# Splits of activations in two steps, scaled groups straight to their parts, and TensorE's operands low in SBUF

## The chip, the core and the metric

The kernel runs on one core of a Trainium2 chip. The metric is the device time of one execution in microseconds (us), the median of several runs. TensorE does the matmuls (PE in the rows), VectorE (DVE) and ScalarE (ACT) work on tiles, GpSimd (POOL) and SyncE (SP) issue DMAs. SBUF is the memory on the chip (128 partitions), PSUM the small memory into which TensorE writes, here as eight banks of 128x512 numbers.

## The reference

One layer for 256 tokens of 2048 features, in float32:

```
h = x + 0.5 * ffn1(rms_norm(x))            # ffn: (silu(u @ w_gate) * (u @ w_up)) @ w_down, inner width 5632
u = rms_norm(h)
z_pool, q, k, v = split(u @ w_in)
a = pool_mixer(z_pool)                     # trailing means of 4 windows, a map for each group, a scale
b = chunk_attention(q, k, v)               # 8 heads, normed q and k, relative bias
ga, gb = sigmoid(u @ w_branch_gate + bias)
h = h + (ga * (a @ w_br_pool) + gb * (b @ w_br_attn)) @ w_out
h = h + 0.5 * ffn2(rms_norm(h))
h = h + sigmoid(rms_norm(h) @ w_ple_gate) * (p @ w_ple)
```

## The kernel before

**Products in parts.** TensorE multiplies a rounded format (fp32r). So each operand is cut into a high part (the rounded value) and a low part (the rest), and a product is three: low activation x high weight (L198), high x high (L200), high x low weight (L205). A weight tile `wraw` of 512 x 512 numbers comes by one DMA of 1 MB; ScalarE casts it to `whi` (L155), VectorE subtracts to `wlo` (L163). For one tile of 128 tokens this is an *item* of 12 matmuls of 512 columns: 4 of L198 and 4 of L200 in turn, then 4 of L205. The activations are the stationary operand, the weight the moving one. Activations are split in the same way by `split` (L113 on ScalarE, L114 on VectorE).

**The stream.** `stream` walks over all items in a written order, and each engine works through its instructions in that order. For item i it writes the load of later weights, `whi` of item i+2, `wlo` of item i+1, and then the 12 matmuls of item i. There are 3 tiles for `whi` and 2 for `wlo`. Ahead of each 12 matmuls `step()` counts down the tasks that were put off with `later(n, task)`: a task with n = 1 is written ahead of the next group of 12.

**Blocks.** In the FFNs four weight tiles and two token tiles make a block of seven products in place of eight (`block`); its left sides are blocks A11 to A22 of the activations and four sums S1 to S4 of them. `Pair` holds these: `uah`/`ual` and `hidah`/`hidal` are the blocks' high and low parts, `ush`/`usl` and `hidsh`/`hidsl` those of the sums. The sums are made on VectorE from `blocks` (L347 to L355) and then split. Groups beyond the first two (b of 2 and 3) need no sums and are `uhi`/`ulo`, `hidhi`/`hidlo`. The up and gate products read u, the down products read hid.

**Norms and turns.** Once a group of 512 features of h is final, `Norm.take` squares it (L539, ScalarE, into a tile `sq`), and two or three groups of 12 later `Norm.turn` transposes it on TensorE into a PSUM tile `tp` (L480), scales it by the norm's gain into `gained` or `blocks` (L529 on ScalarE, four pieces of 128 columns; at the start L520 on VectorE) and splits it. `hid` is transposed in the same way by `turn`. `tp`, `sq`, `gained` and `s3` share a ring of two PSUM banks, so each of them waits until the last reader of the tile before the one before it is done. `h` is updated from the down products by L708 on VectorE; the root of a norm's mean is made by ScalarE and VectorE in `done`.

**Places.** From the tiles' sizes, a partition of SBUF is laid out so (KB of 1000 bytes): rooms of raw weights 17 to 42 and 83 to 107 (there also `merged`, the first half of the operand of w_out, and the first half of the pool's output), whi 42 to 67, wlo 67 to 83, h 107 to 124, u 124 to 169, pieces 169 to 179, and from 180 up to 229 the pools that open and close: hid in an FFN; in the mixer the second half of the pool's output, of the attention's output and of w_out's operand (`mergedl`); the tiles of the last stage.

Of the kernel before, what the change touches and what calls it, by code (L numbers as in the profile page):

```python
# [10 lines left out]
F32 = mybir.dt.float32  # L11
F32R = mybir.dt.float32r
# [4 lines left out]
P = 128  # L17
# [24 lines left out]
def hybrid_block(ctx: ExitStack, tc: tile.TileContext, a: dict, out: bass.AP):  # L42
    nc = tc.nc

    const = ctx.enter_context(tc.tile_pool(name="const", bufs=1))
    wpool = ctx.enter_context(tc.tile_pool(name="wpool", bufs=1))
    act = ctx.enter_context(tc.tile_pool(name="act", bufs=1))
    work = ctx.enter_context(tc.tile_pool(name="work", bufs=1))
    ps_acc = ctx.enter_context(tc.tile_pool(name="ps_acc", bufs=6, space=bass.MemoryType.PSUM))
# [69 lines left out]
    def room(tag, name):  # L119
        assert free[tag] > 0, tag  # L120
        free[tag] -= 1
        return wpool.tile([P, KB, NB], F32, tag=tag, name=name, bufs=ROOMS[tag])

# [142 lines left out]
    class Operand:  # L266
# [14 lines left out]

        def place(self, t):
            return brief_tile("gained")

        def take(self, t, src):
            tt = slice(t * P, (t + 1) * P)
            split(self.hi[:, :, tt], self.lo[:, :, tt], src.rearrange("p (k s) -> p k s", k=KB))
            self.missing -= 1

    class Half:  # L290
# [4 lines left out]
        def __init__(self, pair, b):  # L295
            self.pair, self.b, self.missing = pair, b, NT

        def get(self, k, t):
            xh, xl = self.pair.blocks[self.b, t]
            ks = slice(k * P, (k + 1) * P)  # L300
            return xh[:, ks], xl[:, ks]

        def place(self, t):
            return self.pair.place(self.b, t)

# [3 lines left out]
    class Pair:  # L309
# [18 lines left out]

        def place(self, b, t):
            if self.home is None or b:  # L330
                return brief_tile("gained")
            if self.f is None:
                f = self.home().tile([P, 2, NB], F32, tag="blocks", name="blocks", bufs=1)
                self.f = [f[:, i, :] for i in range(2)]
            return self.f[t]

        def take(self, half, b, t, src):
            if (b, t) in self.blocks:
                split(*self.blocks[b, t], src)
            half.missing -= 1  # L340
            if self.home is None:
                return
            tt = nc.vector.tensor_tensor
            f0, f1 = self.f
            if (b, t) == (0, 1):
                s3 = brief_tile("s3")
                tt(s3, f0, f1, op=ALU.subtract)  # L347
                self.sum(2, s3)
            elif (b, t) == (1, 1):
                tt(f1, f1, src, op=ALU.subtract)  # L350
                self.sum(0, f1)
                tt(f0, f1, f0, op=ALU.subtract)
                self.sum(1, f0)
            elif (b, t) == (1, 0):
                tt(f1, src, f0, op=ALU.add)  # L355
                self.sum(3, f1)
                self.ready = True

        def sum(self, i, src):
# [5 lines left out]
            split(self.sh[:, i, :], self.sl[:, i, :], src)  # L365

# [8 lines left out]
    def block(sides, pair, rest, nr, k0, taken, done2, done1, alone=False):  # L375
# [19 lines left out]
        def form(name):  # L395
            def get():
                while not pair().ready:
                    step()
                return pair().form(name)
            return get  # L400
# [69 lines left out]

    h = [act.tile([P, D], F32, tag=f"h{t}", name=f"h{t}") for t in range(NT)]

# [20 lines left out]
    class Norm:  # L493
# [61 lines left out]
    def load_x(norm, first_weights):  # L555
# [194 lines left out]
    def mixer(norm, following, flat, carry):  # L750
# [8 lines left out]
        def begin():  # L759
            mix = m_["mix"] = inner.enter_context(tc.tile_pool(name="mix", bufs=1))  # L760
            yp = wpool.tile([P, 2, KB, SEQ], F32R, tag="wc", name="ypool", bufs=ROOMS["wc"])
            free["wc"] -= 1
# [146 lines left out]
        def values(hh, pt):  # L909
# [5 lines left out]
            o = y["attn"][hh // KB]  # L915
            split(o.hi[:, hh % KB, :], o.lo[:, hh % KB, :], op[:, :SEQ])
            o.missing -= 1
            if hh == HEADS - 1:
# [38 lines left out]
        def group_map(g, gw, df):  # L957
            for j in range(2):
                yp = ps_tp.tile([P, NB], F32, tag="tp", name="tp")
                for kk in range(2):  # L960
# [7 lines left out]
                nc.scalar.activation(yh, yp[:, :SEQ], AF.Copy, scale=col("pool_scale", c))  # L968
                nc.vector.scalar_tensor_tensor(
                    yl, yp[:, :SEQ], col("pool_scale", c), yh.bitcast(F32),  # L970
                    op0=ALU.mult, op1=ALU.subtract,
                )
                o.missing -= 1
            if g + 1 < POOL_GROUPS:
# [11 lines left out]
        for n in range(D // NB):  # L986
# [28 lines left out]
            def done_attn(accs, g=g, n=n):  # L1015
                if n < 2:
                    tag = ("wa", "wb")[n]
                    free[tag] -= 1
                    both_ = wpool.tile([P, 2, KB, SEQ], F32R, tag=tag, name="merged",
                                       bufs=ROOMS[tag])  # L1020
# [39 lines left out]
    def load_p():  # L1060
# [3 lines left out]
        def turn_p(t, raw):  # L1064
# [4 lines left out]
            tt = slice(t * P, (t + 1) * P)  # L1069
            split(o.hi[:, :, tt], o.lo[:, :, tt], tpv)  # L1070
            o.missing -= 1

# [150 lines left out]
```

## Time and profile before

| | |
|---|---|
| median of 3 runs | 2165.55 us (2165.03 to 2165.77) |
| profiled execution | 2166.04 us, of which the profile's span is 2164.0 |
| TensorE busy | 2088.7 us, 97% of the span, 9206 instructions |
| VectorE busy | 1666.5 us, 77% |
| ScalarE busy | 1156.0 us, 53% |
| read from HBM | 440.44 MB, 204 GB/s over the span |

The stages of the span: FFN1 up to about 700 us, the mixer up to about 1325, FFN2 up to about 1990, then the last norm and the product with the layer's embedding (PLE). In the rows, `out<-in` names the tiles that an instruction writes and reads, with numbers left out, and a bracket gives how long the engine was idle before it and what ended that. The matmuls overlap in the pipeline: one shows 0.39 us or so, while the next starts 0.23 us after it.

### The profile page before, as it was taken

How to read it: one execution, taken by the hardware profiler on the slowest of the kernel's cores; microseconds unless marked ns; L12 is line 12 of the kernel's file. 1: busy time of each engine (PE TensorE's matmuls, PEld its weight loads, DVE VectorE, ACT ScalarE, POOL GpSimd, SP SyncE). 2: the span in 40 equal slices, each digit the busy share in tenths (PEclk: the TensorE clock that was granted, in tenths of full speed). 3: DMA queues.
4: the chain of work that ended last, by engine and by line, in shares of the span. 5: the costliest groups of instructions: out<-in, count | busy, mean ns of one | idle time of the engine just before them, and what ended most of it. 6: DMA issues, size and time to landing. Idle time of an engine off the chain costs nothing. (4 is left out here: it accounts for less than half of the span.)

```text
span 2164.0 us, 22839 instructions
## 1 busy us (share of the span) xinstructions
PE 2088.7 (97%) x9206; PEld 1693.5 (78%) x9206; DVE 1666.5 (77%) x1211; ACT 1156.0 (53%) x1004; POOL 66.0 (3%) x89
## 2 busy tenths in 40 slices
PE   7999999999999899999999999999999999999798
PEld 5878888788887678887888887878788788877576
DVE  5788888888888766554555557898888888888787
ACT  3655456554565743453434356655455555555564
POOL 0000000000000000000000000000000000000000
PEclk9999999999999999999999999999999999999899
DMA  6577577657765655554666556776677567756564
GB/s 224 181 239 227 179 249 243 208 179 259 242 195 171 207 188 192 189 168 159 198 195 195 195 170 192 261 222 204 205 262 230 179 221 255 224 175 215 171 183 156
DMA packets 222441, 444.02 MB, mean 205 GB/s; under 512 B 7480, under 2 KB 7552, under 8 KB 222336
## 3 DMA queue, kind: packets, MB, share of 16 engines
q1 hardware_dynamic: 201968, 400.59, 53.0%
q0 software_dynamic: 20368, 41.98, 10.1%
q8 instruction: 72, 1.18, 0.2%
q14 instruction: 33, 0.27, 0.0%
HBM read 440.44 MB, written 2.10 MB: 204 GB/s over the span
## 5 line engine op out<-in xcount | busy, mean ns | idle before, releaser
L163 DVE TENSOR_TENSOR wlo<-wraw,whi 128x2048 fp32r<-128x2048 f32 (+1 forms) x486 | 1100.8, 2274 | 292.3 <-PE acc L205 144.8
L155 ACT CAST whi<-wraw 128x2048 fp32r<-128x2048 f32 (+1 forms) x486 | 921.0, 1901 | 684.8 <-PE acc L200 185.3
L198 PE MATMUL acc<-whi,ulo 128*128 128x512 f32 x288 | 114.6, 398 | 0.0
L200 PE MATMUL acc<-whi,uhi 128*128 128x512 f32 x288 | 113.3, 393 | 0.0
L198 PE MATMUL acc<-whi,ual 128*128 128x512 f32 x216 | 89.1, 412 | 5.5 <-ACT whi L155 5.5
L200 PE MATMUL acc<-whi,uah 128*128 128x512 f32 x216 | 87.1, 403 | 0.0
L417 DVE TENSOR_TENSOR wraw<-wraw 128x2048 f32<-128x2048 f32 x35 | 80.2, 2292 | 1.2
L413 DVE TENSOR_TENSOR wraw<-wraw 128x2048 f32<-128x2048 f32 x35 | 80.2, 2292 | 1.2
L420 DVE TENSOR_TENSOR wraw<-wraw 128x2048 f32<-128x2048 f32 x35 | 80.0, 2286 | 0.0
L205 PE MATMUL acc<-wlo,uhi 128*128 128x512 f32 x288 | 77.2, 390 | 0.0
L198 PE MATMUL acce<-whi,ulo 128*128 128x512 f32 x184 | 73.2, 398 | 0.0
L198 PE MATMUL accd<-whi,ulo 128*128 128x512 f32 x184 | 72.0, 391 | 0.8 <-ACT p L597 0.8
L200 PE MATMUL acce<-whi,uhi 128*128 128x512 f32 x184 | 71.8, 390 | 0.0
L198 PE MATMUL accb<-whi,usl 128*128 128x512 f32 x184 | 71.8, 390 | 0.0
L198 PE MATMUL acca<-whi,ulo 128*128 128x512 f32 x184 | 71.7, 390 | 0.0
L200 PE MATMUL accd<-whi,uhi 128*128 128x512 f32 x184 | 71.7, 390 | 0.0
L200 PE MATMUL acca<-whi,uhi 128*128 128x512 f32 x184 | 71.7, 390 | 0.0
L200 PE MATMUL accb<-whi,ush 128*128 128x512 f32 x184 | 71.7, 390 | 0.0
L198 PE MATMUL accb<-whi,ual 128*128 128x512 f32 x184 | 71.7, 390 | 0.0
L200 PE MATMUL accb<-whi,uah 128*128 128x512 f32 x184 | 71.6, 389 | 0.0
L198 PE MATMUL accb<-whi,ulo 128*128 128x512 f32 x184 | 71.6, 389 | 0.0
L200 PE MATMUL accb<-whi,uhi 128*128 128x512 f32 x184 | 71.6, 389 | 0.0
(328 smaller groups left out, 4237.6 us busy)
## 6 DMA issues: line engine op xcount, KB each, us to landing
wraw<-in_ffn_w_up_dram SPq DMA_DIRECT2D x88, 1024.0 KB, 7.1
wraw<-in_ffn_w_down_dram SPq DMA_DIRECT2D x88, 1024.0 KB, 9.3
wraw<-in_ffn_w_gate_dram SPq DMA_DIRECT2D x87, 1024.0 KB, 8.8
wraw<-in_w_in_dram SPq DMA_DIRECT2D x32, 1024.0 KB, 5.4
wraw<-in_w_branch_gate_dram SPq DMA_DIRECT2D x32, 1024.0 KB, 5.4
wraw<-in_ffn_w_gate_dram POOLq DMA_DIRECT2D x21, 1024.0 KB, 12.3
wraw<-in_w_out_dram SPq DMA_DIRECT2D x16, 1024.0 KB, 5.0
wraw<-in_w_ple_gate_dram SPq DMA_DIRECT2D x16, 1024.0 KB, 7.6
```

Of the source, the lines that this page charges most:

```text
L155: nc.scalar.copy(out=self.hi[:, ks, :], in_=w.raw[:, ks, :])
L163: nc.vector.tensor_tensor(out=self.lo[:, ks, :], in0=w.raw[:, ks, :], in1=self.hi[:, ks, :].bitcast(F32), op=ALU.subtract,)
L198: nc.tensor.matmul(acc, xl, wh[:, k, :], start=start and k == 0, stop=False, skip_group_check=True)
L200: nc.tensor.matmul(acc, xh, wh[:, k, :], start=False, stop=False, skip_group_check=True)
L205: nc.tensor.matmul(acc, xh, wl[:, k, :], start=False, stop=last and k == len(forms) - 1, skip_group_check=True)
L413: tt(b11.raw, b11.raw, b12.raw, op=ALU.add)
L417: tt(b11.raw, b11.raw, b22.raw, op=ALU.add)
L420: tt(b21.raw, b21.raw, b11.raw, op=ALU.add)
```

## The change

It has three parts.

1. **Splits in two steps.** `split` writes the high part at once, and the low part as a task of `later(1)`, ahead of the next group of 12 matmuls. The counts of missing tiles go down at the low part, and a product waits (by steps) for its own operand's name alone.
2. **Straight to the parts.** Where a scaled group needs no sums (all four groups of the mixer's norm, groups 2 and 3 of the others), ScalarE writes the scaled values into the high part, and VectorE forms the low part from `tp` by four operations of 128 columns (new L568), one step later. `sq`, and at the start `gained`, move from PSUM to the pieces in SBUF. The second of two turns comes two groups of 12 after the first.
3. **Places.** Pools of TensorE's operands stay on the left (whi 17 to 42, wlo 42 to 58, u 58 to 103, the pools that open and close 103 to 153 KB); raw weights, h, pieces, with them `merged` and the first half of the pool's output, go to the right (153 to 229).

```diff
     wpool = ctx.enter_context(tc.tile_pool(name="wpool", bufs=1))
     act = ctx.enter_context(tc.tile_pool(name="act", bufs=1))
-    work = ctx.enter_context(tc.tile_pool(name="work", bufs=1))
+    rawpool = ctx.enter_context(tc.tile_pool(name="rawpool", bufs=1, side="right"))
+    work = ctx.enter_context(tc.tile_pool(name="work", bufs=1, side="right"))
...
-    def split(hi, lo, src):
+    def split(hi, lo, src, then):
         nc.scalar.copy(out=hi, in_=src)
-        nc.vector.tensor_tensor(out=lo, in0=src, in1=hi.bitcast(F32), op=ALU.subtract)
+        def low():
+            nc.vector.tensor_tensor(out=lo, in0=src, in1=hi.bitcast(F32), op=ALU.subtract)
+            then()
+        later(1, low)
     free = dict(ROOMS)
...
         def take(self, half, b, t, src):
+            def sums():
+                half.there()
+                if self.home is None:
+                    return
+                tt = nc.vector.tensor_tensor
+                f0, f1 = self.f
+                if (b, t) == (0, 1):
+                    s3 = brief_tile("s3")
+                    tt(s3, f0, f1, op=ALU.subtract)
+                    self.sum(2, s3)
+                elif (b, t) == (1, 1):
+                    tt(f1, f1, src, op=ALU.subtract)
+                    self.sum(0, f1)
+                    tt(f0, f1, f0, op=ALU.subtract)
+                    self.sum(1, f0)
+                elif (b, t) == (1, 0):
+                    def last():
+                        tt(f1, src, f0, op=ALU.add)
+                        self.sum(3, f1, self.end)
+                    later(1, last)
             if (b, t) in self.blocks:
...
+                split(*self.blocks[b, t], src, sums)
+            else:
+                later(1, sums)
...
+        def there(self, name):
+            return self.ready if name[0] == "S" else not self.halves[int(name[2]) - 1].missing
...
-            f = self.u[b].place(t)
-            if early:
-                nc.vector.tensor_tensor(
-                    out=f.rearrange("p (j s) -> p j s", j=KB),
-                    in0=tp.rearrange("p (j s) -> p j s", j=KB),
-                    in1=col(self.gain, b * KB, KB).unsqueeze(2).to_broadcast([P, KB, P]),
-                    op=ALU.mult,
-                )
-            else:
+            u = self.u[b]
+            gains = [col(self.gain, b * KB + j) for j in range(KB)]
+            if early or (self.home and b < 2):
+                f = u.place(t) if b == 0 else (piece_tile if early else brief_tile)("gained")
+                if early:
+                    nc.vector.tensor_tensor(
+                        out=f.rearrange("p (j s) -> p j s", j=KB),
+                        in0=tp.rearrange("p (j s) -> p j s", j=KB),
+                        in1=col(self.gain, b * KB, KB).unsqueeze(2).to_broadcast([P, KB, P]),
+                        op=ALU.mult,
+                    )
+                else:
+                    for j in range(KB):
+                        js = slice(j * P, (j + 1) * P)
+                        nc.scalar.activation(f[:, js], tp[:, js], AF.Copy, scale=gains[j])
+                u.take(t, f)
+                return
+            hi, lo = u.part(t)
+            tpk = tp.rearrange("p (j s) -> p j s", j=KB)
+            for j in range(KB):
+                nc.scalar.activation(hi[:, j, :], tpk[:, j, :], AF.Copy, scale=gains[j])
+            def low():
                 for j in range(KB):
-                    js = slice(j * P, (j + 1) * P)
-                    nc.scalar.activation(
-                        f[:, js], tp[:, js], AF.Copy, scale=col(self.gain, b * KB + j)
+                    nc.vector.scalar_tensor_tensor(
+                        lo[:, j, :], tpk[:, j, :], gains[j], hi[:, j, :].bitcast(F32),
+                        op0=ALU.mult, op1=ALU.subtract,
                     )
-            self.u[b].take(t, f)
+                u.there()
+            later(1, low)
...
             for t in range(NT):
-                sq = ps_tp.tile([P, NB], F32, tag="tp", name="sq")
+                sq = piece_tile("sq")
...
-                later(2 + i, lambda t=t: self.turn(b, t))
+                later(2 + 2 * i, lambda t=t: self.turn(b, t))
...
-        later(6, turn_vectors(
+        later(4, turn_vectors(
```

**VectorE at the start.** Rows of VectorE's order of instructions from its first on; before (`ual`, `hidsl` and `usl` are low parts of u's first group, `wlo` those of weights):

```order
L75 COPY vcol<-tp 128x16
L520 TENSOR_TENSOR blocks<-tp,vcol 128x512
L114 TENSOR_TENSOR ual<-blocks,uah 128x512
L520 TENSOR_TENSOR blocks<-tp,vcol 128x512
L114 TENSOR_TENSOR hidsl<-blocks,hidsh 128x512
L347 TENSOR_TENSOR s_136<-blocks 128x512
L114 TENSOR_TENSOR usl<-s_136,ush 128x512
L163 TENSOR_TENSOR wlo<-wraw,whi 128x1024 x2
L163 TENSOR_TENSOR wlo<-wraw,whi 128x2048 x2
L520 TENSOR_TENSOR gained<-tp,vcol 128x512
```

and now, where L549 was L520, L171 was L163 and L119 was L114:

```order
L77 COPY vcol<-tp 128x16
L549 TENSOR_TENSOR blocks<-tp,vcol 128x512 x2
L171 TENSOR_TENSOR wlo<-wraw,whi 128x1024 x2
L171 TENSOR_TENSOR wlo<-wraw,whi 128x2048
L119 TENSOR_TENSOR ual<-blocks,uah 128x512
L119 TENSOR_TENSOR hidsl<-blocks,hidsh 128x512
L360 TENSOR_TENSOR s_168<-blocks 128x512
L119 TENSOR_TENSOR usl<-s_168,ush 128x512
L171 TENSOR_TENSOR wlo<-wraw,whi 128x2048
```

The low parts of u now stand behind three low parts of weights, two of them of half a weight.

**VectorE where the up products of a part give way to the down products.** Before, with L350, L352, L355 the sums and L114 the low parts behind each:

```order
L163 TENSOR_TENSOR wlo<-wraw,whi 128x2048 x2
L114 TENSOR_TENSOR hidal<-tp,hidah 128x512
L350 TENSOR_TENSOR blocks<-blocks,tp 128x512
L114 TENSOR_TENSOR hidsl<-blocks,hidsh 128x512
L352 TENSOR_TENSOR blocks<-blocks 128x512
L114 TENSOR_TENSOR hidsl<-blocks,hidsh 128x512
L163 TENSOR_TENSOR wlo<-wraw,whi 128x2048
L114 TENSOR_TENSOR hidal<-tp,hidah 128x512
L355 TENSOR_TENSOR blocks<-tp,blocks 128x512
L114 TENSOR_TENSOR hidsl<-blocks,hidsh 128x512
L163 TENSOR_TENSOR wlo<-wraw,whi 128x2048
L594 TENSOR_TENSOR p_837<-p_837,accb 128x512
```

and now, the sums being L363, L365, L369:

```order
L171 TENSOR_TENSOR wlo<-wraw,whi 128x2048 x3
L119 TENSOR_TENSOR hidal<-tp,hidah 128x512
L363 TENSOR_TENSOR blocks<-blocks,tp 128x512
L365 TENSOR_TENSOR blocks<-blocks 128x512
L119 TENSOR_TENSOR hidal<-tp,hidah 128x512
L119 TENSOR_TENSOR hidsl<-blocks,hidsh 128x512 x2
L171 TENSOR_TENSOR wlo<-wraw,whi 128x2048
L369 TENSOR_TENSOR blocks<-tp,blocks 128x512
L636 TENSOR_TENSOR p_840<-p_840,accb 128x512
L171 TENSOR_TENSOR wlo<-wraw,whi 128x2048
L446 TENSOR_TENSOR wraw<-wraw 128x2048
```

No low part stands directly behind its sum any more; the low part of the last sum stands behind a weight's low part and a sum of weights (L446).

**VectorE at the handover from FFN2 to PLE.** Before, L708 being the updates of h and `s_12970` a sum of u's blocks:

```order
L413 TENSOR_TENSOR wraw<-wraw 128x2048
L347 TENSOR_TENSOR s_12970<-blocks 128x512
L114 TENSOR_TENSOR usl<-s_12970,ush 128x512
L708 SCALAR_TENSOR_TENSOR h_79<-acca,h_79 128x512
L708 SCALAR_TENSOR_TENSOR h_80<-accb,h_80 128x512
L163 TENSOR_TENSOR wlo<-wraw,whi 128x2048
L708 SCALAR_TENSOR_TENSOR h_79<-accb,h_79 128x512
L163 TENSOR_TENSOR wlo<-wraw,whi 128x2048
L417 TENSOR_TENSOR wraw<-wraw 128x2048
L114 TENSOR_TENSOR ual<-gained,uah 128x512
L350 TENSOR_TENSOR blocks<-blocks,gained 128x512
```

and now, where L750 was L708, L360 was L347, L363 was L350:

```order
L439 TENSOR_TENSOR wraw<-wraw 128x2048
L119 TENSOR_TENSOR ual<-blocks,uah 128x512
L750 SCALAR_TENSOR_TENSOR h_82<-acca,h_82 128x512
L750 SCALAR_TENSOR_TENSOR h_83<-accb,h_83 128x512
L171 TENSOR_TENSOR wlo<-wraw,whi 128x2048
L750 SCALAR_TENSOR_TENSOR h_82<-accb,h_82 128x512
L171 TENSOR_TENSOR wlo<-wraw,whi 128x2048
L443 TENSOR_TENSOR wraw<-wraw 128x2048
L360 TENSOR_TENSOR s_13039<-blocks 128x512
L171 TENSOR_TENSOR wlo<-wraw,whi 128x2048
L119 TENSOR_TENSOR ual<-gained,uah 128x512
L363 TENSOR_TENSOR blocks<-blocks,gained 128x512
```

The updates of h moved ahead of the sum, and the sum behind two weights' low parts and a sum of weights (L443).

## Rows read from the trace of the kernel before

**Rows 1.** The page's line of engines: busy us, share of the span, instructions.

```profile
PE 2088.7 (97%) x9206; PEld 1693.5 (78%) x9206; DVE 1666.5 (77%) x1211; ACT 1156.0 (53%) x1004; POOL 66.0 (3%) x89
```

**Rows 2.** What TensorE waited for: us in total, times, longest us.

```profile
PE acce L205 <- DVE wlo L163: 15.3, 10, 3.0
PE tp L480 <- ACT sq L539: 11.7, 8, 4.8
PE tp L480 <- ACT gained L529: 7.5, 7, 2.1
PE acca L205 <- DVE wlo L163: 6.4, 6, 1.1
PE tp L480 <- DVE gained L520: 6.3, 3, 2.6
...
PE tp L73 <- DVE gained L520: 1.5, 1, 1.5
```

**Rows 3.** Stretches: length, each engine's busy us, TensorE's clock, DMA share, GB/s.

```profile
485.00:570.00 85.00, 85.00 (x367) 68.39 (x367) 72.64 (x43) 43.78 (x25) 2.56 (x2) 1.00 0.70 223
700.00:730.00 30.00, 23.68 (x106) 17.64 (x105) 25.43 (x20) 22.62 (x35) 1.30 (x1) 1.00 0.96 306
730.00:762.00 32.00, 28.82 (x130) 22.14 (x129) 24.50 (x25) 22.89 (x33) 2.92 (x5) 1.00 0.36 115
1990.00:2035.00 45.00, 33.56 (x132) 25.55 (x131) 34.99 (x29) 26.44 (x40) 1.28 (x1) 0.85 0.51 163
2035.00:2076.00 41.00, 34.43 (x141) 26.20 (x140) 32.29 (x29) 28.13 (x41) 2.46 (x3) 0.92 0.66 212
```

**Rows 4.** TensorE's timeline (start us, us, line, op), operands u, then hid.

```profile
43.08 0.39 PE L198 MATMUL acc<-whi,ual 128*128 128x512 f32 x1
...
45.80 0.39 PE L198 MATMUL acc<-whi,ual 128*128 128x512 f32 x1
...
245.87 0.39 PE L198 MATMUL acca<-whi,hidlo 128*128 128x512 f32 x1
...
248.67 0.39 PE L198 MATMUL accb<-whi,hidlo 128*128 128x512 f32 x1
```

**Rows 5.** Tiles merged and mergedl: ns min/median/max, first and last start.

```profile
L200 PE MATMUL acc<-whi,merged x64: 387/392/398, 1230.5 to 1310.3; 128*128 128x512 f32 x64
...
L200 PE MATMUL acc<-whi,mergedl x64: 392/396/399, 1242.4 to 1321.5; 128*128 128x512 f32 x64
```

**Rows 6.** List by line: the matmuls on hid, first and last group.

```profile
L198 PE MATMUL accb<-whi,hidal 128*128 128x512 f32 x96 | 38.2, 398 | 0.0
...
L205 PE MATMUL acc<-wlo,hidsh 128*128 128x512 f32 x8 | 2.2, 396 | 0.0
```

**Rows 7.** The start: the second weight's DMA (last number: us to landing), TensorE's timeline.

```profile
wraw<-in_ffn_w_up_dram SPq DMA_DIRECT2D x1, 1024.0 KB, 8.7
...
12.95 0.80 PE L198 MATMUL acc<-whi,ual 128*128 128x512 f32 x1 [5.46 <-ACT whi L155]
...
25.34 0.63 PE L198 MATMUL acc<-whi,ual 128*128 128x512 f32 x1
25.77 0.63 PE L200 MATMUL acc<-whi,uah 128*128 128x512 f32 x1
```

**Rows 8.** Timeline, idle time before and releaser in brackets: 126 to 140, and 2010.

```profile
129.07 0.69 DVE L114 TENSOR_TENSOR hidsl<-blocks,hidsh 128x512 fp32r<-128x512 f32 x1 [0.69 <-ACT hidsh L113]
...
138.78 1.21 PE L205 MATMUL acca<-wlo,uah 128*128 128x512 f32 x4 [1.06 <-DVE wlo L163]
...
2010.14 1.11 PE L480 MATMUL tp<-ident,h 128*128 128x128 f32 x4 [4.76 <-ACT sq L539]
```

**Rows 9.** List by line and shape: busy us, mean ns, idle before.

```profile
L155 ACT CAST whi<-wraw 128x2048 fp32r<-128x2048 f32 x480 | 915.0, 1911 | 684.8 <-PE acc L200 185.3 <-DVE wraw L420 143.7 <-PE accb L200 105.0
...
L163 DVE TENSOR_TENSOR wlo<-wraw,whi 128x2048 fp32r<-128x2048 f32 x480 | 1093.6, 2287 | 286.0 <-PE acc L205 144.8 <-PE accd L205 54.1 <-issue 54.0
...
L969 DVE SCALAR_TENSOR_TENSOR ypoollo<-tp,vcol,ypoolhi 128x256 fp32r<-128x256 f32 x4 | 1.8, 480 | 5.7 <-ACT ypoolhi L968 5.7
```

More of the change, by code (lines that the diff above doesn't have):

```diff
@@ L121, in room @@
         free[tag] -= 1
-        return wpool.tile([P, KB, NB], F32, tag=tag, name=name, bufs=ROOMS[tag])
+        return rawpool.tile([P, KB, NB], F32, tag=tag, name=name, bufs=ROOMS[tag])
     class Weight:
@@ L280, in get, with part, there @@
             return self.hi[:, k, tt], self.lo[:, k, tt]
-        def place(self, t):
-            return brief_tile("gained")
+        def part(self, t):
+            tt = slice(t * P, (t + 1) * P)
+            return self.hi[:, :, tt], self.lo[:, :, tt]
+        def there(self):
+            self.missing -= 1
         def take(self, t, src):
-            tt = slice(t * P, (t + 1) * P)
-            split(self.hi[:, :, tt], self.lo[:, :, tt], src.rearrange("p (k s) -> p k s", k=KB))
-            self.missing -= 1
+            split(*self.part(t), src.rearrange("p (k s) -> p k s", k=KB), self.there)
     class Half:
@@ L296, in __init__, with part, there @@
             self.pair, self.b, self.missing = pair, b, NT
+        def part(self, t):
+            return [x.rearrange("p (k s) -> p k s", k=KB) for x in self.pair.blocks[self.b, t]]
+        def there(self):
+            self.missing -= 1
         def get(self, k, t):
@@ L303, in place @@
         def place(self, t):
-            return self.pair.place(self.b, t)
+            return self.pair.place(t)
         def take(self, t, src):
@@ L327, in __init__, with place @@
             self.ready = False
-        def place(self, b, t):
-            if self.home is None or b:
-                return brief_tile("gained")
+        def place(self, t):
             if self.f is None:
@@ L337, in take, with end, sum @@
         def take(self, half, b, t, src):
-            if (b, t) in self.blocks:
[L339 to L359, printed above, removed]
+            def sums():
[18 more added lines that the diff above has]
+                    later(1, last)
+            if (b, t) in self.blocks:
+                split(*self.blocks[b, t], src, sums)
+            else:
+                later(1, sums)
+        def end(self):
+            self.ready = True
+        def sum(self, i, src, then=lambda: None):
             if self.sh is None:
@@ L364, in sum @@
                 )
-            split(self.sh[:, i, :], self.sl[:, i, :], src)
+            split(self.sh[:, i, :], self.sl[:, i, :], src, then)
+        def there(self, name):
+            return self.ready if name[0] == "S" else not self.halves[int(name[2]) - 1].missing
         def form(self, name):
@@ L396, in get @@
             def get():
-                while not pair().ready:
+                p = pair()
+                while not p.there(name):
                     step()
-                return pair().form(name)
+                return p.form(name)
             return get
@@ L469, in rsqrt_mean @@
         return r
-    h = [act.tile([P, D], F32, tag=f"h{t}", name=f"h{t}") for t in range(NT)]
+    h = [work.tile([P, D], F32, tag=f"h{t}", name=f"h{t}") for t in range(NT)]
     def token_tiles(b):
@@ L915, in values @@
             o = y["attn"][hh // KB]
-            split(o.hi[:, hh % KB, :], o.lo[:, hh % KB, :], op[:, :SEQ])
-            o.missing -= 1
+            split(o.hi[:, hh % KB, :], o.lo[:, hh % KB, :], op[:, :SEQ], o.there)
             if hh == HEADS - 1:
@@ L968, in group_map, with low @@
                 nc.scalar.activation(yh, yp[:, :SEQ], AF.Copy, scale=col("pool_scale", c))
[L969 to L973, printed above, removed]
+                def low(yp=yp, yl=yl, yh=yh, c=c, o=o):
+                    nc.vector.scalar_tensor_tensor(
+                        yl, yp[:, :SEQ], col("pool_scale", c), yh.bitcast(F32),
+                        op0=ALU.mult, op1=ALU.subtract,
+                    )
+                    o.there()
+                later(1, low)
             if g + 1 < POOL_GROUPS:
@@ L1018, in done_attn @@
                     free[tag] -= 1
-                    both_ = wpool.tile([P, 2, KB, SEQ], F32R, tag=tag, name="merged",
+                    both_ = rawpool.tile([P, 2, KB, SEQ], F32R, tag=tag, name="merged",
                                        bufs=ROOMS[tag])
@@ L1069, in turn_p @@
             tt = slice(t * P, (t + 1) * P)
-            split(o.hi[:, :, tt], o.lo[:, :, tt], tpv)
-            o.missing -= 1
+            split(o.hi[:, :, tt], o.lo[:, :, tt], tpv, o.there)
         for t in range(NT):
```

2 lines of the change are left out of this document (1 added, 1 removed).

## The prediction

> **What bounds the kernel now.** I read the engines' busy line first, then what TensorE waited for, then stretches, then single instructions.
>
> TensorE is busy for 2088.7 of 2164.0 us, VectorE for 77% and ScalarE for 53% [rows 1]. So only two things can make the kernel faster: fewer or shorter waits of TensorE, or a shorter step from one matmul to the next. The profiled execution took 2166.04 us, 0.5 us over the median of the runs; I sum against 2166.04 and take the 0.5 off at the end. The three runs lie within 0.74 us; 0.2% (4.3 us) is about what a measurement of this kernel can tell from no change.
>
> The waits [rows 2] are of three kinds: for a weight's low part from VectorE (15.3 and 6.4 us), for a PSUM bank of the transposes that a square (11.7 us) or a gained tile of ScalarE (7.5 us) still held, and the same for gained tiles of VectorE at the start (6.3 and 1.5 us). They cluster: between 485 and 570 TensorE is busy for 85.00 of 85.00 us, but for 23.68 of 30 and 28.82 of 32 in the first handover, and 33.56 of 45 and 34.43 of 41 in the last, there at a mean clock of 0.85 and 0.92 [rows 3].
>
> **The step from matmul to matmul, and the addresses.** Twelve matmuls with a stationary operand from u take 2.72 us (43.08 to 45.80); twelve with one from hid take 2.80 us (245.87 to 248.67) [rows 4]: 226.7 and 233.3 ns each. What differs is where the operand lies: u between 124 and 169 KB of a partition, hid from 180 KB up. The control is in w_out: its operand lies half in merged (83 to 107 KB), half in mergedl (above 180 KB), with the same code and the same kind of moving operand, and the median matmul takes 392 against 396 ns [rows 5]. So I read an address effect of 6.7 ns with its edge between 169 and 180 KB. The moving operands (42 to 83 KB before, 17 to 58 KB after) are below it in both kernels.
>
> After, hid lies between 103 and 153 KB. Low go 1992 matmuls on hid (30 groups of the list by line, from 96 instructions to 8 [rows 6]) and 432 on mergedl, yattn, one pool part and p, counted in the same list. High go 288, on merged and the other pool part. Net 2136 x 6.7 ns = 14.2 us. In the down products VectorE's cover gets thinner: it is busy for 72.64 of 85 us there [rows 3], and the low part of one item there arrives just in time already. I give 0.2 us back for each of the 12 down blocks: **11.7 us**. Bounds: 0 (the 6.7 ns belong to something else in these stages) and 15.
>
> The Trainium skill speaks against this term: TensorE: Matmul & The Clock Gate, "Back-to-back issue gap", gives a warm gap that follows from the number of columns alone, 512 / 2.4 + 2.5, about 216 ns, with no place for the operand's address. By that rule the term would be 0, and the sum below 11.7 us higher; the two levels of this trace, 226.7 and 233.3 ns, do not agree with a single one.
>
> **The start (0 to 60 us).** Four transposes wait for a bank until VectorE has written a gained tile, which stands behind a weight's low part: 6.3 + 1.5 us [rows 2]. Behind the three long ones TensorE runs at half clock, 0.43 us from matmul to matmul (25.34, 25.77) [rows 7] in place of 0.23, for some nine matmuls each: 27 x 0.2 = 5.2 us. With gained in SBUF the bank is free once VectorE has read it, and the second turn comes 12 matmuls later still, so the waits and their cold stretches go: 13.0 us. Against that, the first low of u now stands behind three low parts of weights on VectorE (first order piece). The second weight is asked for at 3.1 us and lands 8.7 us later [rows 7], then its cast 1.91 and its low 2.29 [rows 9], and u's low 0.69 [rows 8]: the first matmul moves from 12.95 [rows 7] to about 16.7, -3.75. Sum **9.3 us**, bounds 5 (one wait with its cold stretch stays) and 13 (the cast of the second weight isn't waited for).
>
> **Up to down, six times.** VectorE makes a sum, idles 0.69 us until ScalarE has its high part, subtracts, and does that three times [rows 8]; the weight's low queued behind is late, and TensorE waits (1.06 us at 138.78) [rows 8]: 6.4 us in 6 places [rows 2], as gaps between matmuls 1.23 us each. The second order piece shows the lows behind the next weight, so VectorE's 2.07 us of idling go and with them the first wait; the second, on acce a few items later (part of the 15.3 us), stays, since the moved lows stand ahead of that weight. I take 6 x 1.23 = **7.4 us**; bounds 4 and 14 (both waits go).
>
> **FFN1 to mixer.** Lost now: 30 - 23.68 = 6.3 and 32 - 28.82 = 3.2 us [rows 3]. The squares leave PSUM, and ScalarE writes the scaled group straight to its high part (four activations, as now, and no cast after them). I replayed both engines' rows by hand in the new order with the old durations, and find new waits in the first half: 1.65 us for h, whose update stands behind a weight, and 2.4 us for a bank that a low still reads. Gain 6.3 - 4.05 + 3.2 = **5.5 us**, bounds 0 and 9.5. VectorE pays for the direct way: four operations of 128 columns for one of 512. No row has them; of 256 columns one takes 0.48 us [rows 9], so four lie between 0.96 (half of it each) and 1.92 us; I take 1.2, nearer to half, since rows of this engine grow nearly with their columns. That is 0.5 us more for each of 16 turns, where VectorE has slack but for the handovers; the replay has it in.
>
> **FFN2 to PLE.** First half: 45 - 33.56 = 11.4 us lost [rows 3], and by the mean clock of 0.85 some 15 matmuls run at half clock, 0.2 us more each, 3.1 in all. The longest wait is 4.76 us at 2010.14 [rows 8]: VectorE stands at s, which needs ScalarE's gained blocks, and the two updates of h that the squares and transposes need are queued behind it. The third order piece shows these updates ahead of s now. What is late next: this norm still makes sums, so a gained tile keeps its bank until the difference L363 has read it, behind two weights' low parts: 5.4 us, and 1.8 cold. Gain 14.5 - 7.2 = **7.3 us**. Second half: 41 - 34.43 = 6.6 us lost [rows 3]; half of it is the chain of the norm itself (squares, root, scale), which the change doesn't shorten: **3.3 us**. Bounds for both: 3 and 18.
>
> **Rest.** Mixer to FFN2 has a short wait for a gained (its part of the 7.5 us [rows 2]), which goes: **1 us**; the one for a low behind the norm's chain stays. The pool groups' rows stand in the same order around their wait for pool weights: 0. DMA queues issue the same transfers in the same order; the rooms of the weights only lie elsewhere.
>
> **Sum.** 11.7 + 9.3 + 7.4 + 5.5 + 7.3 + 3.3 + 1 = 45.5; 2166.0 - 45.5 - 0.5 = **2120 us**.
>
> **The rivals.** (a) The address pays nothing: what separates hid from u is the stage, since hid is written by ScalarE and VectorE while TensorE reads its neighbours, or the faster pace only uncovers VectorE in the down products. For it: VectorE's 85% there; against it the pair merged and mergedl. 2120 + 11.7 = 2132. By the rule of the page named above it is this one.
> (b) No new wait appears. The list of waits [rows 2] sums to 66 us with its smaller rows; 8 of these stand ahead of the first matmul, and 7.8 are in the 9.3 of the start. So 50 + 9.3 + 14.2 + some 5 of cold matmuls: 2166 - 79 = 2087. Against it: the norm's chain at each handover and the pool weights are not touched.
> (c) Slower: the delayed lows become the new wait. A low used by the next item but one stands behind a whole weight on VectorE, as at the start, where that costs 3.75 us; and TensorE's transposes wait for banks that these lows still read. There are 16 turns straight to parts, the turns of hid and 6 changes from up to down to make it dear. Against the 45 us gained it decides from 12 such places on; at 16 the time would be 2120 + 60 = 2180. For it: two PSUM banks only. Against it: outside the handovers TensorE takes 2.7 us for 12 matmuls and VectorE is idle for 15% or more, and I find four such places, priced above.
> (d) The gains of the handovers fall out (new waits as long as the old), and only addresses, start and changes from up to down pay: 2166 - 28 = 2138.
>
> **Chances.** The forecast, within some 8 us, 0.5 (its own range 2110 to 2127); (a) 0.16; (b) or part of it, under 2107, 0.1; (d) 0.14; between (d) and no change 0.03; no change 0.03; (c) 0.04. Faster by over 0.2% 0.93, within 0.2% 0.03, slower 0.04. The range of 2102 to 2141 holds the forecast, (a) and (d) with half of (b)'s lesser cases.
>
> **What would show it.** Addresses: twelve matmuls on hid in 2.72 us, on merged in 2.80. Start: first matmul near 16.7 us, no half clock between 20 and 56. Up to down: no wait on acca, the one on acce still there six times. Handovers: no wait for squares; one of about 5 us near the first transposes of the last norm. The prediction is wrong if hid stays at 2.80 us, or if the list of waits names lows of activations (L119, L568) often.

## The result

The changed kernel takes 2125.36 us (median of 4 runs, 2123.72 to 2127.95) against 2165.29 us of the kernel before run beside it (2163.65 to 2165.77); the ratio is 0.9819, with a 95% interval of 0.9805 to 0.9834. That is 39.9 us less, where 45.5 were forecast; it lies in the range. The profiled execution took 2124.25 us, its span is 2122.1. One of the ten executions of the run e2 below took 5685.86 us and is in none of the figures.

The page's line of engines of the changed kernel: TensorE is busy for 24 us less than in [rows 1], VectorE and ScalarE for nearly as long as before.

```profile
PE 2064.5 (97%) x9206; PEld 1691.9 (80%) x9206; DVE 1669.0 (79%) x1259; ACT 1143.6 (54%) x988; POOL 66.0 (3%) x89
```

What TensorE waited for in the changed kernel (us in total, times, longest):

```profile
PE acce L213 <- DVE wlo L171: 11.9, 15, 3.6
PE acc L206 <- DVE ual L119: 8.7, 1, 8.7
PE acce L206 <- DVE hidlo L119: 6.5, 2, 3.2
PE tp L506 <- DVE blocks L363: 5.2, 1, 5.2
PE tp L1002 <- DVE yattnlo L119: 2.7, 2, 2.0
...
PE tp L506 <- DVE usl L568: 2.2, 1, 2.2
...
PE tp L506 <- DVE h L750: 1.7, 2, 1.2
PE tp L1002 <- ACT pt L948: 1.1, 1, 1.1
...
PE acca L213 <- DVE wlo L171: 0.8, 1, 0.8
```

Against [rows 2], all waits for squares and for gained are gone. Four of the names that are new stand for a low part of an activation (ual, yattnlo, usl L568 in the mixer's norm) or for a bank that a difference still reads (blocks L363). Small ones are new too, as that of the transposes for an update of h (1.7 us). The wait for hidlo was there before, with 1.7 us in place of 6.5:

```profile
PE acce L198 <- DVE hidlo L114: 1.7, 2, 0.9
```

The order of the 512-column matmuls is the same in both kernels. So the same matmul can be looked up in both timelines; the differences of the starts say where the time went:

| stretch, up to | start before | start after | gained in the stretch | forecast |
|---|---|---|---|---|
| first matmul | 12.95 | 16.19 | -3.2 | -3.75 |
| the 105th (end of the start) | 55.52 | 45.47 | 13.3 | 13.0 |
| end of FFN1's down products | 657.86 | 637.53 | 10.3 | 9.1 |
| mixer's products under way | 759.81 | 734.85 | 4.6 | 5.5 |
| FFN2's products under way | 1338.06 | 1313.10 | 0.0 | 1.9 |
| end of FFN2's last sevens | 1950.17 | 1915.58 | 9.6 | 9.1 |
| end of the profile | 2164.0 | 2122.1 | 7.3 | 10.6 |

(The stretches are those of the two profiled executions, 41.9 us apart in their spans. The forecast's 11.7 us for addresses are split here by the number of matmuls, 5.4 for each FFN and 0.9 for the mixer, and the 7.4 from up to down in two.)

Three readings of the changed kernel's timeline (start us, us, engine, line, operation, idle time in brackets). The first matmul, and two that stand twelve apart on hid:

```profile
16.19 0.77 PE L206 MATMUL acc<-whi,ual 128*128 128x512 f32 x1 [8.74 <-DVE ual L119]
...
210.08 0.39 PE L206 MATMUL acca<-whi,hidal 128*128 128x512 f32 x1
...
212.80 0.39 PE L206 MATMUL accb<-whi,hidsl 128*128 128x512 f32 x1
```

Hid takes 2.72 us for twelve now, where [rows 4] had 2.80. Then the end of FFN1, where TensorE reads the low part of the last hid group right behind its turn:

```profile
662.23 4.48 DVE L171 TENSOR_TENSOR wlo<-wraw,whi 128x2048 fp32r<-128x2048 f32 x2
...
666.63 1.28 DVE L119 TENSOR_TENSOR hidlo<-tp,hidhi 128x512 fp32r<-128x512 f32 x2
...
667.37 0.50 PE L206 MATMUL acce<-whi,hidlo 128*128 128x512 f32 x1 [3.23 <-DVE hidlo L119]
```

The lows, put off, stand behind two weights (4.48 us), and TensorE waits 3.2 us, once in each FFN. And the wait that the prediction's replay found at the last handover (5.4 us forecast):

```profile
1985.56 0.68 DVE L363 TENSOR_TENSOR blocks<-blocks,gained 128x512 f32<-128x512 f32 x1
...
1986.38 1.09 PE L506 MATMUL tp<-ident,h 128*128 128x128 f32 x4 [5.22 <-DVE blocks L363]
```

One thing in this trace speaks against the prediction's reading of addresses. Merged lies above 180 KB now, where matmuls were to be slow, and isn't (ns min/median/max):

```profile
L208 PE MATMUL acc<-whi,merged x64: 389/389/397, 1208.1 to 1286.8; 128*128 128x512 f32 x64
```

The median is 389, where merged had 392 and mergedl 396 in [rows 5].

### The profile page after: what moved, and what is told of

Its sections match the earlier page's. It is cut to its first block, busy times and chain, and to the rows that moved or that the text cites. A ratio compares the mean times of both kernels' runs of the same rounds, so it can differ in the third digit from the quotient of the medians.

```text
span 2122.1 us, 22846 instructions
## 1 busy us (share of the span) xinstructions
PE 2064.5 (97%) x9206; PEld 1691.9 (80%) x9206; DVE 1669.0 (79%) x1259; ACT 1143.6 (54%) x988; POOL 66.0 (3%) x89
## 3 DMA queue, kind: packets, MB, share of 16 engines
q0 software_dynamic: 20368, 41.98, 10.3%
## 4 chain that ended last, share of the span: by engine, by line
PE 81%; DVE 13%; issue 3%; DMA 2%; ACT 1%; POOL 0%; SPq 0%; DVEq 0%; ACTq 0%; POOLq 0%
PE acc L206 8%; PE acc L208 8%; PE acc L213 8%; DVE wlo L171 7%; PE accb L206 7%; PE accb L213 7%; PE accb L208 7%; PE acce L213 5%; PE accd L206 4%; PE accd L208 4%; PE accd L213 4%; PE acca L213 4%; PE acca L206 4%; PE acca L208 4%; DVE wraw L446 4%
## 5 line engine op out<-in xcount | busy, mean ns | idle before, releaser
L171 DVE TENSOR_TENSOR wlo<-wraw,whi 128x2048 fp32r<-128x2048 f32 (+1 forms) x486 | 1099.6, 2274 | 316.3 <-PE acc L213 113.4
L163 ACT CAST whi<-wraw 128x2048 fp32r<-128x2048 f32 (+1 forms) x486 | 922.6, 1902 | 663.6 <-PE acc L208 174.7
L443 DVE TENSOR_TENSOR wraw<-wraw 128x2048 f32<-128x2048 f32 x35 | 80.2, 2292 | 1.2
L446 DVE TENSOR_TENSOR wraw<-wraw 128x2048 f32<-128x2048 f32 x35 | 79.9, 2283 | 0.0
```

What stands on the lines that cost most here:

```text
L163: nc.scalar.copy(out=self.hi[:, ks, :], in_=w.raw[:, ks, :])
L171: nc.vector.tensor_tensor(out=self.lo[:, ks, :], in0=w.raw[:, ks, :], in1=self.hi[:, ks, :].bitcast(F32), op=ALU.subtract,)
L443: tt(b11.raw, b11.raw, b22.raw, op=ALU.add)
L446: tt(b21.raw, b21.raw, b11.raw, op=ALU.add)
```

## The experiments

Twelve runs. The first four are on places, the others on the two steps, the banks and what could still be gained. Each is compared with the kernel before on the same chip (its medians were 2164.67 to 2165.47). The interval of a ratio is some 2 to 4 us to either side, so smaller differences between two runs need a trace: where a sentence below goes by the starts of the same matmuls, it compares the run's trace with that of the changed kernel.

**Places.** The places worked out of the tiles' sizes offered a second theory: in the kernel before, the weights' parts start 32 bytes past a multiple of 64 bytes, and so do u, merged and the first half of the pool's output; hid, mergedl and all that opens behind them start at a multiple of 64. In the changed kernel all of them start 32 past one. So what counts could be how a start lies within 64 bytes.

*e1_hid_32_bytes*, the kernel before with a tile more:

```diff
     h = [act.tile([P, D], F32, tag=f"h{t}", name=f"h{t}") for t in range(NT)]
+    pad = work.tile([P, 8], F32, tag="pad", name="pad", bufs=1)
+    nc.gpsimd.memset(pad, 0.0)
```

> The kernel before, with one tile of 32 bytes more at the end of the work pool, so that hid, mergedl and all that opens behind them start 32 bytes higher (179872 in place of 179840 bytes into a partition) and stay above 180 KB. Theory 1, places (low is fast, the prediction's): nothing changes, twelve matmuls on hid take 2.80 us, the time is 2165 us within 0.2%. Theory 2, 64 bytes: what counts is where an operand starts within 64 bytes against the weights, which all start 32 bytes past a multiple of 64; hid was the only large operand that did not. Twelve matmuls on hid take 2.72 us, and the time falls by some 9 us (2290 steps of 6.7 ns, 15 us at most, less what VectorE gives back): 2153 to 2158 us.

2156.15 us, ratio 0.9958 (0.9941 to 0.9975): 8.8 us less than before, with hid as high as ever. Twelve matmuls on hid take 2.75 us:

```profile
244.99 0.39 PE L198 MATMUL acca<-whi,hidlo 128*128 128x512 f32 x1
...
247.74 0.39 PE L198 MATMUL accb<-whi,hidlo 128*128 128x512 f32 x1
```

Theory 1 falls. The 0.03 us that are left to 2.72 are open (by the tiles' sizes hid starts 64 bytes off the weights modulo 128 here, in the changed kernel it doesn't; that was not tried by itself). So a step is 229 ns in this run, not 226.7, and its 8.8 us are less than what the steps can give.

*e2_u_and_hid_off*, *e3_all_on_64* and *e4_weights_on_64*, the changed kernel with 32 bytes ahead of u, ahead of the weights' parts, and ahead of both (e4: what moves the weights by 32 moves u by 64):

```diff
     make_identity(nc, ident)
+    pad_const = const.tile([P, 8], F32, tag="pad", name="pad", bufs=1)   # e3, e4
+    pad_act = act.tile([P, 8], F32, tag="pad", name="pad", bufs=1)       # e2, e4
```

(and a memset of each).

> The changed kernel, with 32 bytes put ahead of u, so that u, hid and mergedl start at multiples of 64 bytes, the weights at 32 past one, all of them as low as before. Theory 1, places: no change, 2125 us. Theory 2, 64 bytes: nearly every step of 512 columns takes 233.3 ns in place of 226.7, twelve of them 2.80 us; 8200 steps of 6.7 ns are 55 us, less some 10 that now cover waits for VectorE: 2165 to 2180 us. Merged and the first half of the pool's output are untouched and stay at 2.72.

> The changed kernel, with 32 bytes put ahead of the weights' parts, so that weights' parts, u, hid and mergedl all start at multiples of 64 bytes; merged and the first half of the pool's output stay 32 past one. Theory 1, places: no change, 2125 us. Theory 2a (stationary and moving operand have to start alike): 2.72 us for twelve on u and hid, 2.80 on merged; 2125 + 2. Theory 2b (the stationary operand alone has to start 32 past a multiple of 64): 2.80 on u and hid, 2.72 on merged; 2165 to 2180 us.

> The changed kernel, with the weights' parts at multiples of 64 bytes and u, hid and mergedl still 32 past one. Theory 1, places: 2125 us. Theory 2a (both operands have to start alike): all steps at 2.80 us for twelve, 2165 to 2180 us. Theory 2b (the stationary operand alone): all at 2.72, 2125 us.

| run | weights' parts | u, hid | merged | us | ratio to before |
|---|---|---|---|---|---|
| changed kernel | 32 | 32 | 32 | 2125.36 | 0.9819 (0.9805 to 0.9834) |
| e2 | 32 | 0 | 32 | 2165.41 | 1.0003 (0.9994 to 1.0013) |
| e3 | 0 | 0 | 32 | 2126.63 | 0.9826 (0.9812 to 0.9841) |
| e4 | 0 | 32 | 32 | 2166.55 | 1.0005 (0.9996 to 1.0015) |

(Starts are bytes modulo 64, worked out from the tiles' sizes; no trace shows an address.) The tiles hidah and merged in e2 (ns min/median/max):

```profile
L210 PE MATMUL accb<-whi,hidah x96: 392/396/397, 191.4 to 2053.2; 128*128 128x512 f32 x96
L210 PE MATMUL acc<-whi,merged x64: 389/389/397, 1235.1 to 1314.8; 128*128 128x512 f32 x64
```

The same in e3:

```profile
L210 PE MATMUL accb<-whi,hidah x96: 389/389/397, 188.7 to 2015.4; 128*128 128x512 f32 x96
L210 PE MATMUL acc<-whi,merged x64: 392/394/397, 1210.5 to 1290.0; 128*128 128x512 f32 x64
```

And in e4:

```profile
L212 PE MATMUL accb<-whi,hidah x96: 392/395/396, 190.9 to 2052.2; 128*128 128x512 f32 x96
L212 PE MATMUL acc<-whi,merged x64: 392/394/397, 1234.4 to 1314.8; 128*128 128x512 f32 x64
```

The pairs agree: 389 where stationary and moving operand start alike modulo 64, 394 to 396 where they don't, whichever is at 0, and with nothing moved by more than 64 bytes. So theory 2a stands, and 2b falls (e3 would be slow, e4 fast). In the changed kernel the 32 bytes alone are worth 40 to 41 us, as much as the whole change, since they slow nearly all matmuls; in the kernel before, u started like the weights already, and only hid, mergedl and what opens behind them didn't.

**The two steps.** *e5_lows_at_once*, the changed kernel with

```diff
-        later(1, low)
+        low()
```

in `split`:

> The changed kernel, with the low part of each split written at once again, directly behind its high part; the direct way to the parts, the squares and early gained tiles in SBUF, and all places stay as changed. Theory 1 (the two steps are what took away the waits from up to down): they come back, 6 x 2.1 us, as do VectorE's idle 0.69 us per sum; against that the first matmul comes 3.3 us earlier, the two waits of 3.2 us for hidlo at the end of each FFN fall to some 1 us, and the two for yattnlo (2.7 us) go: 2125 + 12.5 - 3.3 - 4.4 - 2.7 = 2127 us. Theory 2 (the two steps carry most of what isn't places): 2135 us or more. Theory 3 (they are a loss by themselves): under 2121 us.

2130.59 us. In this run S3 of the norms in front of the last two stages is made from a block that another sum has already changed, since the sums of a block without parts are still put off; so *e11_lows_at_once_mended* makes these and the last sum at once too:

```diff
-                    later(1, last)
+                    last()
...
-                later(1, sums)
+                sums()
```

> As the run with the lows at once, with the sum of a block that has no parts of its own also made at once, as before the change. Theory 1: as there, 2131 us within 2: the six waits on acca of 1.1 us and the longer ones on acce from up to down are there, with an earlier first matmul. Theory 2 (the order of the sums at the handovers mattered in that run): more than 2 us from 2131.

2131.77 us, ratio 0.9848 (0.9832 to 0.9865). Two rows of e11's list of waits:

```profile
PE acce L213 <- DVE wlo L171: 16.6, 11, 3.6
PE acca L213 <- DVE wlo L171: 7.3, 7, 1.1
```

The waits on acca are back, as in [rows 2] (the seventh, of 0.8 us, stands in the changed kernel too), and e11 is theory 1 of its own. By the starts of the same matmuls in e5 the six changes from up to down cost 1.9 to 2.0 us each, 11.7 in all, and the two steps lose some of that at the three places below: net they are worth 6.4 us. That is theory 1 of e5 in kind, but e5's time is 3.6 us over its figure. What the figure left out is the start: with all lows at once the first matmul comes 3.3 us earlier, but by the 105th matmul e5 is 2.6 us behind the changed kernel.

**The direct way and the banks.** *e6_gained_again*:

```diff
-            if early or (self.home and b < 2):
-                f = u.place(t) if b == 0 else ...
+            if True:
+                f = u.place(t) if b == 0 and self.home else ...
```

> The changed kernel, with scaled groups without sums made as gained in a PSUM bank again, then cast and subtracted in two steps; all else as changed. Theory 1 (the direct way pays at the two handovers and into FFN2, by a bank and a cast of 0.59 us less): waits for gained or its low come back there, 2128 to 2134 us. Theory 2 (VectorE's four small operations cost what the cast had): within 2 us of 2125. FFN1 and the stages between show no difference by either.

2134.83 us, ratio 0.9858 (0.9843 to 0.9872): 9.5 us more than the changed kernel, theory 1 by its size and slightly more, but not by its places: by the starts of the same matmuls 10.4 us are lost at the handover from FFN1 to the mixer, and none at the last handover or into FFN2. *e10_squares_in_psum*:

```diff
-                sq = piece_tile("sq")
+                sq = brief_tile("sq")
```

> The changed kernel, with the squares' tile in a PSUM bank again. Theory 1 (the squares' bank is what the transposes at the handovers waited for, 11.7 us before): waits for sq come back at both handovers, 3 to 8 us: 2128 to 2133 us. Theory 2 (those waits were for h, which the order of VectorE's updates has moved, and the bank was incidental): within 2 us of 2125.

2139.42 us, ratio 0.9883 (0.9869 to 0.9898): 14.1 us more, the largest of the edits to steps and banks; theory 1, but beyond the 3 to 8 us that it gave. By the starts 11.4 us are lost at the handover from FFN1 to the mixer and 5.3 at the last. One row of the list of waits of e6:

```profile
PE tp L506 <- ACT gained L558: 8.5, 2, 4.8
```

and one of e10:

```profile
PE tp L506 <- ACT sq L581: 18.4, 8, 4.5
```

Each of the two costs more at the first handover than the 4.6 us that the whole change gained there, and the waits for sq are longer than before the change (18.4 us, 11.7 in [rows 2]). A reason that fits is that with the turns further apart and the lows put off each bank is held for longer; no run shows it by itself.

*e9_gained_in_sbuf*, the other way:

```diff
-                f = u.place(t) if b == 0 else (piece_tile if early else brief_tile)("gained")
+                f = u.place(t) if b == 0 else piece_tile("gained")
```

> The changed kernel, with the gained tiles of groups with sums (two in front of FFN2, two in front of the last product) in a piece of SBUF in place of a PSUM bank. Theory 1 (the transposes at the last handover wait 5.2 us only because gained keeps its bank until L363 has read it): the wait and the cold matmuls behind it go, 5.2 + 1.6 us, and of this some stays: 2119 to 2122 us. Theory 2 (behind it the weight's low and the norm's chain are as late): the wait moves to wlo or to an operand's low part, 2124 to 2126 us.

2126.26 us, ratio 0.9822 (0.9808 to 0.9837): no gain, theory 2. The wait of 5.2 us on L363 is gone; between 1960 and 2034 us the list of this run's waits has

```profile
PE acce L213 <- DVE wlo L171: 4.7, 2, 3.6
PE accd L206 <- DVE h L750: 1.9, 1, 1.9
PE tp L506 <- DVE h L750: 1.3, 2, 0.8
```

Of the first row, 3.6 us stand in the changed kernel as well; the rest are new and are waits for a weight's low and for updates of h, both VectorE's work. By the starts, 6.7 us are won at one matmul and in the half clock behind it, and 6.1 are lost within the next 25: 3.3 in such waits, the rest since 13 of the 25 now run at half clock (0.43 us from matmul to matmul, 0.23 in the changed kernel; the granted clock is 0.59 from 1990 to 1998 us).

**Lows at once where the product is near.** *e7_first_lows* sets a flag by which `split` makes the low part at once, for the first group only:

```diff
+        if at_once[0]:
+            low()
+        else:
+            later(1, low)
...
+                at_once[0] = early and b == 0
                 u.take(t, f)
+                at_once[0] = False
```

> The changed kernel, with the low parts of u's first group (two tiles at the start) written at once, ahead of the weights' low parts; the sums and all later splits in two steps. Theory 1 (the first matmul waits for nothing but ual behind the second weight's low): it starts at 12.9 us in place of 16.2, and all of that stays: 2122 us. Theory 2 (the weights, not yet landed, take it back in the next items): the start is earlier, the time within 1 us of 2125.

2121.96 us, ratio 0.9800 (0.9786 to 0.9815), 3.4 us less than the changed kernel. The intervals of the two ratios overlap, so the trace has to say it: the first matmul comes 3.5 us earlier, and at the end of FFN1's down products the run is still 4.0 us ahead. That is theory 1. Behind that this one execution loses 3 us again in stretches that the edit doesn't touch; e12, with the same edit, keeps nearly all. The first matmul in this run's timeline:

```profile
12.73 0.80 PE L210 MATMUL acc<-whi,ual 128*128 128x512 f32 x1 [5.87 <-ACT whi L167]
```

*e8_last_lows* sets the same flag for the last hid group of each FFN (`last and j == nblk - 1`):

> The changed kernel, with the last hid group of each FFN split at once (two turns, of which the product reads the low part right behind). Theory 1 (the low stands behind two weights on VectorE, 4.48 us, and TensorE waits 3.2 us for it): both waits fall to some 1 us and the handovers behind them come earlier by as much: 2125 - 4.4 = 2121 us. Theory 2 (VectorE is the pace there, so the wait moves to a weight's low part): a wait for wlo of 2 to 3 us in the same place, within 2 us of 2125.

2117.56 us, ratio 0.9778 (0.9763 to 0.9792), 7.8 us less: theory 1, and more than its 4.4. What theory 1 left out is the clock: in the changed kernel TensorE's granted clock is half behind the wait in FFN2 (0.91 in the mean from 1942 to 1960 us, 1.00 at the same matmuls in e8), so that seven matmuls there take 1.4 us longer than in e8; seven more at half clock in the first handover cost 1.4, of which e8 loses 0.6 again. The row of hidlo in its list of waits:

```profile
PE acce L210 <- DVE hidlo L121: 2.1, 2, 1.0
```

*e12_some_lows_at_once* has both, and the attention's values:

```diff
+            at_once[0] = True
             split(o.hi[:, hh % KB, :], o.lo[:, hh % KB, :], op[:, :SEQ], o.there)
+            at_once[0] = False
```

> The changed kernel with the low parts written at once in three places only: u's first group at the start, the last hid group of each FFN, and the attention's values (whose bank TensorE waits 2.7 us for); everywhere else in two steps. Theory 1 (the three places are independent, each stalls TensorE by itself): the gains of the two single runs add up, 3.4 + 7.8, and some 2 us for the attention: 2112 us. Theory 2 (they share VectorE's slack, or the wait for h at the handover is next): 2115 to 2119 us.

2109.92 us, ratio 0.9748 (0.9731 to 0.9764): 15.4 us less than the changed kernel and 55.5 less than the one before, the fastest here. The wait for yattnlo is gone and ual's is again one for the weight. By the starts of the same matmuls, the beginning gives 3.5 us, the attention 4.1 where 2 were expected, the ends of the two FFNs with their handovers 2.9 and 3.9: what e7 and e8 show singly adds up, so the places are independent. The first rows of its list of waits:

```profile
PE acce L217 <- DVE wlo L175: 11.8, 15, 3.6
PE acc L210 <- ACT whi L167: 5.7, 1, 5.7
PE tp L511 <- DVE blocks L368: 5.2, 1, 5.2
```

## Why the prediction was right, and where not

**Addresses** (11.7 us): right in size by luck, wrong in its mechanism, "an address effect with its edge between 169 and 180 KB". The step that failed is the reading of the control: merged and mergedl differ in height, but also in their start modulo 64 bytes, and only the second counts, by e1 to e4. (Merged's 392 ns in [rows 5] are mixed from uneven steps behind pauses; where its stream runs on, it steps at 226 to 227 ns in that trace too.) The luck is that the change moved hid both lower and to a start like the weights'. The forecast steps of 2.72 us on hid came, those of 2.80 on merged didn't. Taken over the steps in which neither kernel waits (under 0.245 us in both traces), the 2424 matmuls that were to get faster gain 14.2 us, and the 288 that were to get slower lose none; by the forecast's 6.7 ns it would have been 16.2 less 1.9. The waits at hid's matmuls grow by 1.6 us in the two FFNs, where I gave 2.4 back. e1, with its steps of 229 ns, gains 9.9 us in the same matmuls and 8.8 in all. Rival (a), that addresses pay nothing, falls with e1. The rule of the Trainium skill that speaks against the term (TensorE: Matmul & The Clock Gate, "Back-to-back issue gap"), one gap for a number of columns, doesn't hold here: the same matmuls step at 226.7 or 233.3 ns by 32 bytes of place.

**Start** (9.3): 10.1, all steps as forecast: the first matmul at 16.19 (16.7 forecast), the waits and their half clock gone: between 21 and 56 us TensorE is now busy throughout and its clock is 1.00, where it was busy for 27.20 us at 0.85 (stretch, busy us of each engine, clock; before, then after):

```profile
21.00:56.00 35.00, 27.20 (x108) 21.49 (x107) 21.06 (x23) 14.43 (x18) 0.00 (x0) 0.85 0.51 175
...
21.00:56.00 35.00, 35.00 (x166) 28.65 (x165) 23.86 (x25) 21.78 (x32) 0.00 (x0) 1.00 0.65 225
```

The banks are not all of it: with the lows at once (e5) only 7.4 of the 13.3 us behind the first matmul are left.

**Up to down** (7.4): under-sized. The wait on acca went as forecast, and the one on acce, which was to stay, fell by a third as well (0.87 us at 133.20, where it was 1.36): 1.9 us in each of the six places, 11.6 in all, by the starts of the same matmuls. e5 shows the size from the other side, 11.7.

**FFN1 to mixer** (5.5): 4.6. The bank that a low still reads (usl L568) costs 2.2 us, 2.4 forecast. What I missed is hidlo ahead of it, 3.2 us in place of about 1. The four operations of 128 columns that I put at 1.2 us take 0.34 each, 1.37 for a turn: this engine's rows grow less with their columns than I took (0.34, 0.48 and 0.69 us for 128, 256 and 512).

**FFN2 to PLE** (7.3 + 3.3): 7.3. The new wait on L363 was found and sized rightly (5.2, forecast 5.4); hidlo is missed here too. The two waits for hidlo more than cover the shortfall of 0.9 and 3.3 us at the handovers: e8 gives 7.8 us back.

**Mixer** (1, with 0.9 of addresses): 0.0. The prediction looked at the pool's lows and not at the attention's, whose bank is also held for 12 matmuls longer: yattnlo 2.7 us, pt 1.1 in place of 0.3, together 4.1 by the starts of the same matmuls. The steps on mergedl, yattn and the pool part gave 2.5 us here, merged and its half of the pool lost nothing, and the short wait into FFN2 went; so the 0.0 is a gain and a loss of one size.

So rival (c) was at work, but at three places in place of twelve: ual (3.2), hidlo (4.4 by its waits) and yattnlo (2.7). The prediction's own sign of being wrong, lows of activations often in the list of waits, came in part: six waits. Rivals (b) and (d) fall: new waits came, and the handovers did pay. e6 and e10 show that the first handover hangs on the direct way and on the squares in SBUF, the last on the squares (5.3 of its 7.3 us), and e9 that one bank more would have added nothing. That the sum came within 6 us owes something to luck too: up to down is 4.2 us over its figure, the mixer and the two handovers 6.1 under theirs.

## What to carry to other kernels

Put off the part of a chain that another engine still has to make, so that an engine doesn't idle for its neighbour; but where the product stands next in the order, make it at once, since put off it stands behind whatever long instruction comes between (two weights, 4.48 us). A PSUM ring of two banks shared by four kinds of tile is dear (one tile back in it cost 14.1 us here): what TensorE doesn't write, such as a square that nobody reads, belongs elsewhere. And where a trace shows two levels for one kind of matmul, test the place of its operands by a pad of 32 bytes: it costs one line, and tells height from alignment.

## What the runs showed of the hardware

A matmul of 512 columns in fp32r steps at 226.7 ns (2.72 us for twelve, changed kernel) when its stationary and its moving operand start alike modulo 64 bytes of a partition, and at 233.3 ns (2.80 us, hid in the kernel before) when one is 32 bytes off. Height doesn't matter in these runs: merged above 180 KB took 389 ns in the changed kernel, hid at 103 to 153 KB 396 in e2. Nor does it matter which of the two is at the multiple of 64: e2 and e4 lose all of the changed kernel's 40 us by it, e3 nothing beyond noise (1.3 us). The rule is not the whole of it: in e1, alike modulo 64 but 64 bytes apart modulo 128, a step on hid took 229 ns. Why is not shown; how it goes for other offsets was not tried.
